# Batch norm with ReLU on one core: which two rows are computed in two parts

## The chip, the cores and the metric

One core of a Trainium2 chip. The metric is device microseconds of one execution. The traced span of an execution, from its first to its last instruction, is about 1.7 us shorter than its time (82.0 against 83.68); one kernel below (e1) differs.

## The reference

```python
def reference(x, gamma, beta, running_mean, running_var, eps):   # x: (32, 128, 32, 32) float32
    normalized = (x - running_mean[None, :, None, None]) / np.sqrt(running_var[None, :, None, None] + eps)
    scaled = normalized * gamma[None, :, None, None] + beta[None, :, None, None]
    return np.maximum(scaled, 0).astype(np.float32)
```

x is 16.78 MB; it is read once and a result of the same size is written once.

## The kernel before

x is seen as two halves t, each of 128 partitions times 16 rows j times 1024 elements. The 16 rows of a partition are 64 KB that lie together in memory. All of x fits on the chip, so every tile has a place of its own and no buffer is reused. `TILES` lists the tiles as (half, first row, end row). A tile is one load, except that the second half is loaded in two (`LOAD_CUTS`), and one store, except that the first tile is stored row by row (`STORE_CUTS`).

```python
J = 16
TILES = ((0, 0, 2), (0, 2, 4), (0, 4, 8), (0, 8, 16), (1, 0, 16))
LOAD_CUTS = {(1, 8)}
STORE_CUTS = {(0, 1)}
HALVES = {(0, 0), (0, 1)}
# ...
    tiles = []
    for t, a, b in TILES:                          # six loads, all issued from SP
        xt = data.tile([P, b - a, HW], F32, name=f"x{t}_{a}")
        cuts = [a] + [j for j in range(a + 1, b) if (t, j) in LOAD_CUTS] + [b]
        for c, d in zip(cuts, cuts[1:]):
            nc.sync.dma_start(out=xt[:, c - a : d - a, :], in_=xr[t, :, c:d, :])
        tiles.append((t, a, b, xt))
# ... the parameters: four tiny loads, a matmul that spreads them, sqrt, reciprocal, scale_t, bias_t
    with tc.manual_schedule(engines={mybir.EngineType.Activation}):
        for t, a, b, xt in tiles:
            first = a
            for j in range(a, b):
                step = HW // 2 if (t, j) in HALVES else HW
                for w in range(0, HW, step):
                    nc.scalar.activation(
                        out=xt[:, j - a, w : w + step], in_=xt[:, j - a, w : w + step],
                        func=ACTF.Relu, bias=bias_t[:, j : j + 1], scale=scale_t[:, j : j + 1],
                    )
                if j + 1 == b or (t, j + 1) in STORE_CUTS:
                    nc.scalar.dma_start(
                        out=outr[t, :, first : j + 1, :], in_=xt[:, first - a : j + 1 - a, :]
                    )
                    first = j + 1
```

So ACT (ScalarE) computes every row and also issues the six stores; SP issues the six loads.

## Time and profile before

| | before |
|---|---|
| time, median of 3 (range) | 83.6 us (83.53 to 83.6) |
| span of the profiled run | 82.0 us |
| ACT busy | 39.1 us (48%) |
| load queue q1, store queue q10, share of the 16 DMA engines' span | 48.7%, 47.6% |
| bytes read, written | 16.78 MB, 16.78 MB |

The prediction below shows the lines that carry the reading. (A load brings data from memory to the core, a store takes it back; 16 DMA engines move both. A packet is the unit that the trace records: here one partition's stretch of a transfer, 4 to 64 KB, and a few very small ones.) A queue's share times the span is the time that each DMA engine spent on that queue's packets: 48.7% of 82.0 is 39.9 us for loads, 47.6% is 39.0 us for stores, and the rest, 3.0 us, is time in which the engine had no packet. **Span = loads + stores + rest** is an account in which a lost microsecond must show up in one of three columns. (Shares are printed to 0.1%, so loads and stores are each good to 0.05 us and the rest to 0.1. Packets overlap a little in the records, which show up to 16.8 of 16 engines busy at a time.)

Two lines of the list of DMA issues and one of the waits give the slack behind ACT (the last number of an issue is the time from issue to landing; for a wait: total, times, longest, in us):

```profile
out_dram<-x ACTq DMA_DIRECT2D x1, 4096.0 KB, 28.7
out_dram<-x ACTq DMA_DIRECT2D x1, 25.1
...
ACT x L102 <- DMA x<-in_x_dram: 7.6, 3, 2.9
```

The first is the 4 MB store, the second the last store, whose size is not printed.

### The profile page before, as it was taken

How to read it: one execution, taken by the hardware profiler on the slowest of the kernel's cores; microseconds unless marked ns; L12 is line 12 of the kernel's file. 1: busy time of each engine (PE TensorE's matmuls, PEld its weight loads, DVE VectorE, ACT ScalarE, POOL GpSimd, SP SyncE). 2: the span in 40 equal slices, each digit the busy share in tenths (PEclk: the TensorE clock that was granted, in tenths of full speed). 3: DMA queues.
4: the chain of work that ended last, by engine and by line, in shares of the span. 5: the costliest groups of instructions: out<-in, count | busy, mean ns of one | idle time of the engine just before them, and what ended most of it. 6: DMA issues, size and time to landing. Idle time of an engine off the chain costs nothing.

```text
span 82.0 us, 120 instructions
## 1 busy us (share of the span) xinstructions
PE 0.7 (1%) x2; PEld 0.5 (1%) x2; DVE 0.8 (1%) x5; ACT 39.1 (48%) x36; POOL 0.8 (1%) x6
## 2 busy tenths in 40 slices
PE   0002000000000000000000000000000000000000
PEld 0002000000000000000000000000000000000000
DVE  0000300000000000000000000000000000000000
ACT  0600477799239999199994199993000000000000
POOL 3000000000000000000000000000000000000000
DMA  2899997979899989999799799998992999996590
GB/s 48 336 424 456 416 544 336 524 322 526 338 434 430 506 358 506 390 434 444 320 460 500 316 424 448 512 432 368 480 736 128 416 512 512 512 512 288 224 512 0
DMA packets 1792, 33.56 MB, mean 409 GB/s; under 512 B 256, under 2 KB 256, under 8 KB 512
## 3 DMA queue, kind: packets, MB, share of 16 engines
q1 hardware_dynamic: 864, 16.78, 48.7%
q10 hardware_dynamic: 928, 16.78, 47.6%
HBM read 16.78 MB, written 16.78 MB: 409 GB/s over the span
## 4 chain that ended last, share of the span: by engine, by line
DMA 56%; ACT 10%; issue 2%; SPq 0%
DMA x<-in_x_dram 56%; ACT x L102 10%; SPq L56 0%
## 5 line engine op out<-in xcount | busy, mean ns | idle before, releaser
L102 ACT ACTIVATE x<-x,bias_t,scale_t 128x1024 f32<-128x1024 f32 (+1 forms) x34 | 37.5, 1177 | 9.9 <-DMA x<-in_x_dram 7.6
L86 ACT ACT_TABLE_LOAD x1 | 1.3, 1283 | 2.6 <-issue 2.6
L86 ACT ACTIVATE std_t<-cols,eps_t 128x16 f32<-128x16 f32 x1 | 0.3, 273 | 4.5 <-PE cols L78 4.5
L78 PE MATMUL cols<-raw,rep 8*128 8x64 f32 x2 | 0.7, 429 | 7.6 <-DMA raw<-in_beta_dram 7.6
L78 PEld LDWEIGHTS cols<-raw,rep 8*128 8x128 f32 x2 | 0.5, 306 | 7.6 <-issue 7.6
L68 POOL TENSOR_SCALAR_AFFINE_SELECT rep<-rep 8x128 f32<-8x128 f32 x1 | 0.4, 392 | 0.1
L88 DVE RECIPROCAL rstd_t<-std_t 128x16 f32<-128x16 f32 x1 | 0.3, 254 | 7.7 <-ACT std_t L86 7.7
L67 POOL MEMSET rep<- 8x128 f32 x1 | 0.2, 194 | 0.3 <-POOLq L130 0.3
L90 DVE TENSOR_TENSOR scale_t<-cols,rstd_t 128x16 f32<-128x16 f32 x1 | 0.2, 175 | 0.1
L92 DVE TENSOR_TENSOR ms_t<-cols,scale_t 128x16 f32<-128x16 f32 x1 | 0.2, 175 | 0.0
L94 DVE TENSOR_TENSOR bias_t<-cols,ms_t 128x16 f32<-128x16 f32 x1 | 0.2, 174 | 0.0
L130 POOL MEMSET const-bfloat16-1.0<- 128x1 bf16 x1 | 0.1, 106 | 0.0
L130 POOL MEMSET const-uint8-127<- 128x1 uint8 x1 | 0.1, 106 | 0.0
L130 POOL MEMSET const-float32-0.0<- 128x1 f32 x1 | 0.1, 103 | 0.3 <-issue 0.3
L130 POOL MEMSET const-float32-1.0<- 128x1 f32 x1 | 0.1, 103 | 0.0
L65 DVE MEMSET eps_t<- 128x1 f32 x1 | 0.1, 59 | 0.9 <-PEq L130 0.9
## 6 DMA issues: line engine op xcount, KB each, us to landing
x<-in_x_dram SPq DMA_DIRECT2D x3, 4096.0 KB, 38.7
out_dram<-x ACTq DMA_DIRECT2D x1, 4096.0 KB, 28.7
x<-in_x_dram SPq DMA_DIRECT2D x2, 1024.0 KB, 5.8
x<-in_x_dram SPq DMA_DIRECT2D x1, 2048.0 KB, 11.3
out_dram<-x ACTq DMA_DIRECT2D x1, 2048.0 KB
out_dram<-x ACTq DMA_DIRECT2D x2, 512.0 KB, 19.6
out_dram<-x ACTq DMA_DIRECT2D x1, 1024.0 KB
raw<-in_running_var_dram ACTq DMA_DIRECT2D x1, 0.5 KB
```

The source lines that it names most:

```text
L65: nc.vector.memset(eps_t, float(eps))
L67: nc.gpsimd.memset(rep, 1.0)
L68: nc.gpsimd.affine_select(out=rep, in_=rep, compare_op=mybir.AluOpType.is_equal, fill=0.0, base=0, pattern=[[0, P // Q], [-1, Q]], channel ...
L78: nc.tensor.matmul(cols.rearrange("p k j -> p (k j)"), rep.rearrange("q r s -> q (r s)"), raw.rearrange("q k j -> q (k j)"), start=True, s ...
L86: nc.scalar.activation(out=std_t, in_=cols[:, 0, :], func=ACTF.Sqrt, bias=eps_t[:, 0:1], scale=1.0)
L88: nc.vector.reciprocal(out=rstd_t, in_=std_t)
L90: nc.vector.tensor_mul(out=scale_t, in0=cols[:, 1, :], in1=rstd_t)
L92: nc.vector.tensor_mul(out=ms_t, in0=cols[:, 2, :], in1=scale_t)
L94: nc.vector.tensor_sub(out=bias_t, in0=cols[:, 3, :], in1=ms_t)
L102: nc.scalar.activation(out=xt[:, j - a, w : w + step], in_=xt[:, j - a, w : w + step], func=ACTF.Relu, bias=bias_t[:, j : j + 1], scale=sc ...
L130: nc = _bacc.Bacc("TRN2", target_bir_lowering=False, num_devices=1)
```

## The change

The two split rows move from the start of ACT's work to the middle of it. In itself the split costs ACT time; at the start it delays the first stores, in the second half it stands ahead of a wait for a load. The numbers that are computed stay the same.

```diff
-HALVES = {(0, 0), (0, 1)}
+HALVES = {(1, 0), (1, 1)}
```

## The prediction

> **What bounds the kernel now.** I read the page's slices first, then its queue lines, then the timeline of ScalarE (ACT), the DMA windows, and last the waits. The kernel does one fused scale, bias and relu per row of x on ACT, in place, between a stream of loads on one DMA queue (q1) and a stream of stores on another (q10). From the page of the kernel before (busy tenths in 40 slices of about 2.05 us, then the queues with packets, MB and the share of the 16 DMA engines' span):
>
> ```profile
> ACT  0600477799239999199994199993000000000000
> DMA  2899997979899989999799799998992999996590
> q1 hardware_dynamic: 864, 16.78, 48.7%
> q10 hardware_dynamic: 928, 16.78, 47.6%
> ```
>
> The DMA row is nearly full from the second slice to the last but two. The two queues add up to 96.3% of 82.0 us, which is 79.0 us of work for each engine, so only 3.0 us are left without a packet. ACT has 39.1 us of work (48%) and nothing at all in the last twelve slices. Is the 3.0 us at the ends or in the middle? From the windows (columns: stretch, its length, busy times of five engines, clock, DMA share, GB/s):
>
> ```profile
> 0.00:2.20 2.20, 0.00 (x0) 0.00 (x0) 0.06 (x1) 0.00 (x0) 0.80 (x6) 1.00 0.30 56
> 2.20:11.20 9.00, 0.66 (x2) 0.50 (x2) 0.78 (x4) 3.07 (x4) 0.00 (x0) 1.00 1.00 420
> 11.20:46.90 35.70, 0.00 (x0) 0.00 (x0) 0.00 (x0) 26.87 (x25) 0.00 (x0) 1.00 1.01 426
> 46.90:81.10 34.20, 0.00 (x0) 0.00 (x0) 0.00 (x0) 9.12 (x8) 0.00 (x0) 1.00 0.98 423
> 81.10:82.00 0.90, 0.00 (x0) 0.00 (x0) 0.00 (x0) 0.00 (x0) 0.00 (x0) 1.00 0.00 0
> ```
>
> At the ends: the start (2.2 us at a share of 0.30, so about 1.5 us idle) and the last 0.9 us. In the three stretches between, the share is 1.00, 1.01 and 0.98 (a packet seems to be booked whole where it starts, hence the 1.01 and the uneven tenths of short slices), and the rate is 420, 426 and 423 GB/s whether only loads run, both run, or only stores run. So the DMA engines never starve between 2.2 and 81.1 us, and how loads and stores are mixed changes the rate by under 2%. **The bound is bytes over DMA rate**: 33.56 MB at about 425 GB/s is 79 us, plus the two ends.
>
> Now where ACT stands against this, in the timeline (start, length, then work and, in brackets, the idle time before it and what ended it):
>
> ```profile
> 9.61 1.52 ACT L102 ACTIVATE x<-x,bias_t,scale_t 128x512 f32<-128x512 f32 x2 [1.02 <-DVE bias_t L94]
> 11.16 0.37 ACTq L110 DMA_DIRECT2D out_dram<-x  x1
> 11.58 1.52 ACT L102 ACTIVATE x<-x,bias_t,scale_t 128x512 f32<-128x512 f32 x2 [0.45 <-ACT x L102]
> 13.13 0.37 ACTq L110 DMA_DIRECT2D out_dram<-x  x1
> ...
> 23.91 9.16 ACT L102 ACTIVATE x<-x,bias_t,scale_t 128x1024 f32<-128x1024 f32 x8 [2.94 <-DMA x<-in_x_dram]
> ...
> 34.85 9.16 ACT L102 ACTIVATE x<-x,bias_t,scale_t 128x1024 f32<-128x1024 f32 x8 [1.78 <-DMA x<-in_x_dram]
> 46.87 9.16 ACT L102 ACTIVATE x<-x,bias_t,scale_t 128x1024 f32<-128x1024 f32 x8 [2.86 <-DMA x<-in_x_dram]
> 56.05 0.34 ACTq L110 DMA_DIRECT2D out_dram<-x  x1
> ```
>
> (Left out: rows 2 to 7 of the first half with their stores at 15.95 and 21.00, and the 4 MB store at 33.10.) Three times ACT waits for a load: before 23.91, 34.85 and 46.87. Those waits, 2.94 + 1.78 + 2.86 = 7.6 us, are the total that the view of waits gives. They are cushions: ACT work that grows or shrinks ahead of one is taken up by it. The last store is issued at 56.05. The list of DMA issues gives the 4 MB store ahead of it, issued at 33.10, a landing 28.7 us later, at 61.8. So the store queue has work for 61.8 - 56.1 = 5.7 us more when the last store joins it; that store lands 25.1 us after its issue, at 81.2, and the rest of the span is the closing.
>
> **What the Trainium skill says.** "DMA: Bandwidth & Descriptors", section "Where 436 GB/s comes from", puts a ceiling of 435.2 GB/s on the 16 ports; the trace's 420 to 426 agrees that little is left. The same page, section "Queues, rings and completion order", says that each DMA engine goes round its queues packet by packet. The trace agrees: 864 packets on q1 are 6 loads x 128 partitions plus 6 x 16 small ones, so a packet is one partition's run (8, 16 or 32 KB for loads, 4 to 64 KB for stores). While both run, the first 24 store packets of an engine (8 x 4, 8 x 4, 8 x 8 KB) facing 24 load packets of 32 KB would give 768 to 128 KB, 6 to 1; the queue view for 11.2 to 46.9 us has 12.88 MB loaded and 2.33 MB stored, 5.5 to 1. "ScalarE: Activation LUTs", section "What ACT_TABLE_LOAD costs", gives 280 ns + 0.833 ns per element for an ACTIVATE with one pointer operand and about 93 ns more for a second (ours has scale and bias): 800 ns at 512 and 1226 ns at 1024. The groups by form show 805 and 1227 ns on average. It agrees.
>
> **The change part by part.** The two rows split into two instructions of 512 elements become rows 0 and 1 of the second half of x; instruction count, bytes, transfers and buffers stay as they are.
>
> Removed at the front: a pair of halves takes 1.52 us, one whole row 1.23 us, so 0.29 us less for row 0 and the same for row 1. The first store should be issued at 11.16 - 0.29 = 10.87, the second at 13.13 - 0.58 = 12.55, the third (rows 2 and 3) at 15.95 - 0.58 = 15.37 and the fourth (rows 4 to 7) at about 20.4. No load holds these back: the 2 MB load of rows 4 to 7 is issued by 2.3 us and lands 11.3 us later, by 13.6, while its rows would start at 15.76. Then ACT waits for the load of rows 8 to 15 as before; the 2.94 us wait becomes about 3.5. The 0.58 us ends there.
>
> Added at the back: inside a run of rows, a row adds (9.16 - 1.23) / 7 = 1.13 us; a half adds 1.52 - 0.81 = 0.71, so a split row 1.42. Two of them make the run that starts at 34.85 longer by 2 x 0.29 = 0.58 us: it ends at 44.6 instead of 44.0. The load that lets the last eight rows go arrives at 46.87, so the wait shrinks from 2.86 to about 2.3. There is no store between rows 7 and 8 of that half, so nothing is issued later. The last store goes out at 56.05 as before.
>
> DMA: starting stores 0.3 to 0.6 us earlier moves at most a round or so of store packets forward. One round is a 4 or 8 KB packet, 0.15 or 0.30 us at 425/16 = 26.6 GB/s for an engine. Loads may therefore land up to 0.3 us later, the last run may start at 46.9 to 47.2, and the last store be issued at 56.1 to 56.4, still over 5 us before the store queue is empty. What moves forward in the store queue is paid back after the loads end. Sum on the path that sets the end: 0.0 us. Sum of ACT busy time: -0.58 + 0.58 = 0.
>
> **The rivals.** First, the front sets the time: each store that leaves earlier shortens everything after it. That would make 83.6 - 0.6 = 83.0 us (-0.7%). For it: the first store can't start before ACT. Against it: the engines are full with loads meanwhile (share 1.00 from 2.2 to 11.2 us), so an earlier store only displaces a load. Second, the back sets the time: the extra 0.58 us reaches the last store and the end, 84.2 us (+0.7%). For it: the chain of waits does run through the last eight ACT rows. Against it: two cushions, 2.86 us and 5.7 us, each larger than 0.58. Third, the mixing: stores that join earlier change how reads and writes interleave, and mixed traffic is slower or faster. Against it: 420, 426 and 423 GB/s in the three stretches; a shift of 0.6 us at a rate that differs by 1.5% is 0.01 us. I see no engine that could become the bound: ACT stays at 39.1 us.
>
> **Range and chances.** The working says no change, so 83.6 us. The three times of before lie between 83.53 and 83.6 and the profiled run took 83.68, so the scatter is about 0.1 us; I widen to 83.3 to 83.9 for chip-to-chip scatter and for half of either of the first two rivals. Even a rival in full is 0.7%, far inside 2%: within 2% has 0.98, the other two 0.01 each.
>
> **What would show it right or wrong.** Right: the first store issued near 10.9, the wait before the rows 8 to 15 of the first half about 0.6 us longer, that before the last eight rows 0.3 to 0.6 us shorter, their start at 46.8 to 47.2, the last store issued before 56.5 and landing near 81.2, queue shares still 96 to 97%, ACT busy 39.1 us. Wrong: an idle DMA stretch in the middle, a start of the last rows moved by more than 0.5 us, a last store that leaves after the 4 MB store has landed, or a store-only rate other than 423 GB/s with all else the same; the last would mean that how loads and stores meet costs time, the term that I put at zero.

## The result, and the profile after

The changed kernel took 83.51 us (median of 6, 83.44 to 83.59) and the kernel before 83.56 us (median of 6, 83.48 to 83.71). The ratio was 0.9993 with a 95% interval of 0.998 to 1.0006: no change. (A ratio is the mean time of one kernel's runs over the mean of the other's of the same rounds, so it is not quite the ratio of the medians quoted.) The output was correct.

From the page of the changed kernel (busy tenths in 40 slices, then the queues):

```profile
ACT  0600477799039999199998099993000000000000
DMA  2899999999989898969789699996993899999090
q1 hardware_dynamic: 864, 16.78, 48.5%
q10 hardware_dynamic: 928, 16.78, 47.7%
```

From its timeline (start, length, work, idle time before it):

```profile
9.63 1.24 ACT L102 ACTIVATE x<-x,bias_t,scale_t 128x1024 f32<-128x1024 f32 x1 [1.02 <-DVE bias_t L94]
10.90 0.37 ACTq L110 DMA_DIRECT2D out_dram<-x  x1
11.32 1.24 ACT L102 ACTIVATE x<-x,bias_t,scale_t 128x1024 f32<-128x1024 f32 x1 [0.45 <-ACT x L102]
12.59 0.37 ACTq L110 DMA_DIRECT2D out_dram<-x  x1
...
23.85 9.16 ACT L102 ACTIVATE x<-x,bias_t,scale_t 128x1024 f32<-128x1024 f32 x8 [3.42 <-DMA x<-in_x_dram]
...
34.92 9.71 ACT L102 ACTIVATE x<-x,bias_t,scale_t 128x512 f32<-128x512 f32 x10 [1.92 <-DMA x<-in_x_dram]
46.91 9.16 ACT L102 ACTIVATE x<-x,bias_t,scale_t 128x1024 f32<-128x1024 f32 x8 [2.27 <-DMA x<-in_x_dram]
56.09 0.34 ACTq L110 DMA_DIRECT2D out_dram<-x  x1
```

And from its waits and its list of issues (the last store):

```profile
ACT x L102 <- DMA x<-in_x_dram: 7.6, 3, 3.4
```

```profile
out_dram<-x ACTq DMA_DIRECT2D x1, 25.0
```

The reader is to see the 0.55 us wander. It leaves the front: the second store goes out at 12.59 in place of 13.13 us. It is swallowed by the first wait, 3.42 in place of 2.94 us. It comes back in the second half: that group of ten instructions (four halves and six rows, listed under its first form) takes 9.71 in place of 9.16 us. It is swallowed again by the last wait, 2.27 in place of 2.86 us. The total of the three waits is 7.6 us in both kernels, the last rows start at 46.91 against 46.87, the last store leaves at 56.09 against 56.05 and lands at 81.1 against 81.2. The account is 39.7 + 39.1 + 3.1 us against 39.9 + 39.0 + 3.0.

### The profile page after: what moved, and what is told of

Its sections match the earlier page's. It is cut to its first block, busy times and chain, and to the rows that moved or that the text cites. A ratio compares the mean times of both kernels' runs of the same rounds, so it can differ in the third digit from the quotient of the medians. Undisturbed runs are those within 1.5% of the kernel's fastest.

```text
span 81.9 us, 120 instructions
## 1 busy us (share of the span) xinstructions
PE 0.7 (1%) x2; PEld 0.5 (1%) x2; DVE 0.8 (1%) x5; ACT 39.1 (48%) x36; POOL 0.8 (1%) x6
## 4 chain that ended last, share of the span: by engine, by line
DMA 56%; ACT 10%; issue 2%; SPq 0%
DMA x<-in_x_dram 56%; ACT x L102 10%; SPq L56 0%
## 5 line engine op out<-in xcount | busy, mean ns | idle before, releaser
L102 ACT ACTIVATE x<-x,bias_t,scale_t 128x1024 f32<-128x1024 f32 (+1 forms) x34 | 37.5, 1178 | 9.9 <-DMA x<-in_x_dram 7.6
```

What stands on the lines that cost most here:

```text
L102: nc.scalar.activation(out=xt[:, j - a, w : w + step], in_=xt[:, j - a, w : w + step], func=ACTF.Relu, bias=bias_t[:, j : j + 1], scale=sc ...
```

## The experiments

That nothing happened is weak evidence for a reason: a change that could not matter and one that was absorbed look the same. So the experiments make ACT's delay large, put it where one cushion or the other must take it, and move the stores in time. The theory is that of the prediction: the time is the DMA engines' packets plus their idle time, and ACT has cushions. The rivals are that the front sets the time, that the back does, and that how loads and stores meet costs time. All diffs are against the changed kernel. Ratios are to the kernel before, run on the same chip. All outputs were correct.

The account of every profiled run, from its shares and span, with the mean length of its 32 KB load packets, worked out from the packet records of the trace:

| run | time, median us | ratio (95%) | loads + stores + rest = span | 32 KB load packet, mean (longest) us |
|---|---|---|---|---|
| before, first profile | 83.56 | | 39.9 + 39.0 + 3.0 = 82.0 | 1.233 (1.46) |
| changed, first profile | 83.51 | 0.9993 (0.998 to 1.0006) | 39.7 + 39.1 + 3.1 = 81.9 | 1.223 (1.48) |
| e1_no_halves | 83.99 | 1.0032 (1.0005 to 1.006) | 39.8 + 39.0 + 3.3 = 82.1 | 1.232 (1.57) |
| e2_halves_last_rows | 83.57 | 0.9983 (0.9956 to 1.001) | 39.8 + 39.1 + 3.0 = 81.9 | 1.234 (1.43) |
| e3_front_16 | 84.19 | 1.0057 (1.002 to 1.0094) | 40.2 + 39.1 + 3.1 = 82.4 | 1.253 (1.67) |
| e4_last_rows_16 | 87.77 | 1.0486 (1.0452 to 1.0519) | 39.8 + 39.2 + 7.1 = 86.1 | 1.229 (1.40) |
| e5_back_16 | 84.69 | 1.0129 (1.0107 to 1.0152) | 39.6 + 39.1 + 4.1 = 82.9 | 1.224 (1.46) |
| e6_stores_late | 84.39 | 1.0095 (1.0072 to 1.0118) | 40.4 + 39.0 + 3.2 = 82.7 | 1.258 (2.04) |
| e7_big_both | 83.87 | 1.0031 (1.0012 to 1.0051) | 39.6 + 38.8 + 3.9 = 82.3 | 1.219 (1.33) |
| e8_front_16_stores_late | 84.25 | 1.0079 (1.006 to 1.0098) | 40.2 + 39.1 + 3.1 = 82.4 | 1.244 (1.91) |
| e9_big_cut | 85.06 | 1.0186 (1.0166 to 1.0206) | 40.6 + 38.8 + 3.8 = 83.2 | 1.287 (2.43) |
| e10_after_again | 83.55 | 1.0007 (0.9988 to 1.0027) | 39.9 + 39.0 + 3.3 = 82.2 | 1.230 (1.55) |
| e11_before_again | 83.93 (one look) | | 39.8 + 39.0 + 3.4 = 82.2 | 1.229 (1.83) |
| e12_one_store_late | 85.14 | 1.0193 (1.0176 to 1.021) | 39.5 + 38.9 + 5.2 = 83.6 | 1.214 (1.22) |

### e1_no_halves: no split at all

```diff
-HALVES = {(1, 0), (1, 1)}
+HALVES = set()
```

> No row is split: the front as in the changed kernel, the back as in the kernel before, so ACT has two fewer instructions and 0.58 us less work than either. Theory (DMA bytes bound, ACT changes absorbed by waits): same time as both, 83.5 us within 0.2; last store issued near 56.1; the wait before the last eight rows back to about 2.85 us. Rival front (earlier first stores shorten the run, and the changed kernel paid that back by its later halves): 83.0 us, that is -0.6.

Measured: 83.99 us against 83.78 for before, whose eleven runs spread from 83.44 to 84.0. Less work came out 0.3% slower, and the expected 83.5 was missed. But the traced spans of its six runs lie between 81.8 and 82.1 us, on average 81.95, against 82.03 for the eleven runs of before. What is longer is the difference of time and span: 2.02 to 2.09 us in all six runs, where every run of every other kernel has 1.66 to 1.76. So the split rows cost or save nothing in the span, and this program has about 0.34 us more outside the span, of which the trace shows nothing. The rival front (83.0 us) is refuted at its own size: the front was as in the changed kernel, the back as in the kernel before, and the span did not shrink by 0.6. The last store left at 56.05 us and the wait before the last rows was 2.84 us, as expected.

### e2_halves_last_rows: the split behind the last wait

```diff
-HALVES = {(1, 0), (1, 1)}
+HALVES = {(1, 8), (1, 9)}
```

> The two split rows are rows 8 and 9 of the second half, after the last wait for a load, where only the store queue's backlog (5.7 us) can absorb them. Theory: last store issued 0.58 us later than in the changed kernel, 56.7 us, the time unchanged, 83.5 within 0.2, the last store landing at the same 81.1. Rival back: +0.58 us, 84.1.

From its timeline and its list of issues:

```profile
46.94 9.71 ACT L102 ACTIVATE x<-x,bias_t,scale_t 128x512 f32<-128x512 f32 x10 [2.96 <-DMA x<-in_x_dram]
56.68 0.34 ACTq L110 DMA_DIRECT2D out_dram<-x  x1
```

```profile
out_dram<-x ACTq DMA_DIRECT2D x1, 24.4
```

The last store left 0.6 us later, at 56.68, took 0.6 us less to land (24.4 in place of 25.0) and landed at the same 81.1 us. Time 83.57 us. This is the second cushion at work alone: the store waits in its queue behind the 4 MB store anyway.

### e4_last_rows_16 and e5_back_16: more than the cushions hold

e4 splits rows 8 and 9 of the second half, e5 rows 0 and 1 of it (no change to `HALVES`), in 16 parts each:

```diff
-HALVES = {(1, 0), (1, 1)}
+HALVES = {(1, 8), (1, 9)}            # e4 alone
-                step = HW // 2 if (t, j) in HALVES else HW
+                step = HW // 16 if (t, j) in HALVES else HW
```

> Rows 8 and 9 of the second half in 16 parts each: 8.7 us more ACT work after the last wait for a load, a dose beyond the 5.7 us of backlog. Theory: last store issued near 64.8, after the store queue has run dry at about 61.7; the DMA engines idle from there until the last store's first packet, some 1.4 us after its issue (the first load's packets come that long after its issue), so 4.5 us of idle DMA in the middle and a time of 88.0, with 1 us either way. If the backlog were no real cushion: +8.7, 92.2. If ACT were not on the path at all: 83.5.

> Rows 0 and 1 of the second half (the rows the change picked) in 16 parts each: 8.7 us more than whole rows, ahead of the last wait for a load. Theory: that wait (2.85 us with whole rows) goes to zero, the last eight rows start 5.8 us late at 52.7, the last store leaves at 61.9, its first packet about 1.1 us later (64.5 to 65.6 us in the run with rows 8 and 9 in 16 parts), 63.0, against a store queue dry at 61.7: 1.3 us of idle DMA, time 84.8 us, between 84.3 and 85.5. Without the first cushion it would be the 87.8 of that other run.

The timeline of e4 and its windows (stretch, length, busy times, clock, DMA share, GB/s):

```profile
46.89 17.57 ACT L102 ACTIVATE x<-x,bias_t,scale_t 128x64 f32<-128x64 f32 x38 [2.81 <-DMA x<-in_x_dram]
64.49 0.34 ACTq L110 DMA_DIRECT2D out_dram<-x  x1
```

```profile
62.00:65.00 3.00, 0.00 (x0) 0.00 (x0) 0.00 (x0) 2.46 (x3) 0.00 (x0) 1.00 0.00 0
```

The timeline of e5:

```profile
34.80 26.54 ACT L102 ACTIVATE x<-x,bias_t,scale_t 128x64 f32<-128x64 f32 x46 [1.80 <-DMA x<-in_x_dram]
61.37 0.34 ACTq L110 DMA_DIRECT2D out_dram<-x  x1
```

The dose is nearly the same, 8.4 us (17.57 less 9.16) in e4. In e4 only the store queue's backlog can take it, and in the 3 us shown no packet starts: the engines are dry while ACT is still computing. (By the packet records none moves from 61.50 to 65.33 us.) In e5 the wait for the load is gone (rows 0 to 15 run as one group of 26.54 us), and the last store leaves at 61.37 us, just as the queue runs dry. Measured 87.77 and 84.69 us, expected 88.0 and 84.8. In the account both add to the rest alone: 4.0 to 4.1 us and 1.0 to 1.1 us. So both cushions are real, and what exceeds them was paid in idle DMA time. Their sizes follow: in e4 the backlog took 8.4 - 4.0 = 4.4 us; in e5, whose dose is 8.3 us (26.54 less 18.24 for sixteen whole rows, as e3 below shows), the wait of 2.8 us and the backlog took 8.3 - 1.1 = 7.2, which leaves 4.4 again. The wait has the size read before; the backlog is smaller than the 5.7 us read from its landing, because its last packet had ended by 61.5 us and the last store's first packet started only 0.84 us after its issue. (The two expectations had allowed 1.4 and 1.1 us for this.) The rival back is true only beyond the cushions; for the change's 0.55 us it is refuted.

### e3_front_16: a large delay at the front

```diff
-HALVES = {(1, 0), (1, 1)}
+HALVES = {(0, 0), (0, 1)}
-                step = HW // 2 if (t, j) in HALVES else HW
+                step = HW // 16 if (t, j) in HALVES else HW
```

> Rows 0 and 1 of the first half in 16 parts each. A part of 64 costs about 0.34 us (from 1.13 us a row and 0.71 a half in a run: 0.29 fixed and 0.05 for 64 elements), so each row 5.5 us in place of 1.13 and ACT is 8.7 us later at the front. Theory: the three waits for loads (3.4, 1.9, 2.3 us, 7.6 in all) take up 7.6 us, the last rows start about 1.1 us later, near 48, the last store leaves near 57.2, still before the backlog ends: time unchanged, 83.5 within 0.3. Rival front: a delay of the first store is paid, +8.7 us, 92; if stores that start later only lengthen the store-only stretch at the same rate, nothing.

Its timeline and its queues:

```profile
29.37 9.18 ACT L102 ACTIVATE x<-x,bias_t,scale_t 128x1024 f32<-128x1024 f32 x8 [0.42 <-ACT x L102]
...
38.96 18.24 ACT L102 ACTIVATE x<-x,bias_t,scale_t 128x1024 f32<-128x1024 f32 x16 [0.41 <-ACT x L102]
57.23 0.34 ACTq L110 DMA_DIRECT2D out_dram<-x  x1
```

```profile
q1 hardware_dynamic: 864, 16.78, 48.8%
q10 hardware_dynamic: 928, 16.78, 47.4%
```

All three waits for loads are gone, and the last store leaves at 57.23 us, 1.1 us later, as expected. The time was to stay; it was 84.19 us, 0.6% above before. The 8.5 us of delay were not paid, so the rival front is refuted again, but 0.4 us were. The account puts them in the loads: 40.2 us, with the rest still 3.1. No engine idled in the middle; the load packets took longer, most of it (0.5 us for each engine above 1.21 us a packet, by the packet records) between 40 and 44 us, just after the 4 MB store was issued at 38.58 us.

### e6_stores_late and e8_front_16_stores_late: the first half's stores held back

e6 (e8 uses `(0, 15)` in place of `(1, 4)`, and has the front in 16 parts as e3):

```diff
+        held = []
         for t, a, b, xt in tiles:
# ...
-                    nc.scalar.dma_start(out=..., in_=...)
+                    if t == 0:
+                        held.append((outr[t, :, first : j + 1, :], xt[:, first - a : j + 1 - a, :]))
+                    else:
+                        nc.scalar.dma_start(out=..., in_=...)
                     first = j + 1
+                if (t, j) == (1, 4):
+                    for o, i in held:
+                        nc.scalar.dma_start(out=o, in_=i)
```

> The five stores of the first half are held back by up to 27 us, until row 4 of the second half is done, near 37.6 us, so that loads run almost alone (to about 42 us) and then stores almost alone. Theory (bytes over rate, when a store starts doesn't matter while the engines have packets): 83.5 us within 0.3, no idle DMA. Rival front: 83.5 + 27 = 110. Rival mixing (loads and stores in turn slow each other, as the 0.4 us of the run with the front in 16 parts suggests, where load packets of 32 KB took 1.25 us in place of 1.22): about 0.3 to 0.5 us faster, 83.1.

> The front in 16 parts as in the run that came out at 84.2, but the five first-half stores held until row 15 of the first half is done, near 37.3 us. If the 0.4 us there came from ACT's delay as such: 0.4 above the run with held stores and unsplit front. If it came from how store packets met load packets: the same as that run, within 0.2 us, and load packets of 32 KB at 1.22 us on average, not 1.25.

From the timeline of e6, and its DMA view for 38.5 to 42.0 us; then the same view of the changed kernel (queue, packets, MB, share of the 16 engines in that stretch):

```profile
32.39 0.86 ACTq L120 DMA_DIRECT2D out_dram<-x  x2
```

```profile
q1 hardware_dynamic: 32, 1.05, 98.1%
q10 hardware_dynamic: 32, 0.13, 9.1%
```

```profile
q1 hardware_dynamic: 47, 1.54, 101.9%
q10 hardware_dynamic: 33, 0.27, 18.2%
```

Two expectations failed. First, the place: the stores were issued from 32.39 us, not 37.6, when the first of the second half's rows had just started: here the issue ran ahead of the ACT instructions before it in the program. In e8 the stores went out from 22.81 us, ahead of the ACT work in the same way, but not before their own rows were done (the 4 MB store at 36.03, its last row at 36.00). The first store packets came at 14.4 to 14.8 us in before, 19.0 to 19.5 in e3, 26.5 to 27.0 in e8 and 36.0 to 36.5 in e6. Second, the sign: holding the stores back was neither free nor a gain but cost 0.95% in e6 and 0.8% in e8. Some 22 us of delay of the first store cost 0.8 us, so the front is still not the bound. And e8, with 8.5 us more ACT work ahead of the stores, is not slower than e6. But its stores also went out earlier than those of e6, and its load packets averaged 1.244 us, not the expected 1.22, so the pair does not separate ACT's delay from the meeting of loads and stores as planned.

What does cost shows in the fences. In 3.5 us e6 took 32 load packets of 32 KB for 98.1% of 16 engines' time: 0.981 x 3.5 x 16 / 32 = 1.72 us each. The changed kernel took 47 in the same stretch: 1.019 x 3.5 x 16 / 47 = 1.21 us each, though it moved more store bytes beside them. The slow packets came late: beside the first store packets, at 36.3 to 38.5 us, load packets still took 1.21 to 1.28. Over the run the mean packet is 1.258 us in e6 against 1.23 in four looks at the two kernels. An engine has 24 such packets, so that is 24 x 0.03 = 0.7 us of the 0.8. (In e8 it is 24 x 0.015 = 0.4 us of 0.7.)

### e7_big_both and e9_big_cut: fewer, larger transfers

```diff
-TILES = ((0, 0, 2), (0, 2, 4), (0, 4, 8), (0, 8, 16), (1, 0, 16))
+TILES = ((0, 0, 16), (1, 0, 16))
-STORE_CUTS = {(0, 1)}
+STORE_CUTS = set()                   # e9: {(0, 12)}
-HALVES = {(1, 0), (1, 1)}
+HALVES = set()
```

> First half loaded in one 64 KB packet a partition and stored likewise, second half as it was, no split rows. Packets took 0.34 us (8 KB load), 0.61 (16 KB), 1.22 (32 KB), and 0.16, 0.31, 0.61, 1.21 (4 to 32 KB stores) against 2.42 for 64 KB; per engine 8 of each: loads save about 0.7 us, stores 0.3. ACT starts at 21.5 and the first store leaves near 40, when the loads are nearly done; the last store leaves near 59 against a first store that ends near 60, so no idle expected, but little room. Theory: 82.6 us, 0.9 below the changed kernel, between 82.2 and 83.2. If an early first store mattered (rival front): 83.5 + 29 or so.

> The kernel with 64 KB loads of the first half, but its store is cut after row 11, so that the first store is issued near 36.5 us and not at 41.1. In the uncut kernel the loads were done about 0.5 us before the first store's packets came, and its DMA engines had 78.5 us of packets in 79.2 us: 0.7 us idle. Theory (bytes over rate, idle costs one for one): the idle goes, 83.2 us, 0.6 below the uncut kernel and 0.3 below the changed kernel. Rival mixing: the one or two rounds in which loads and stores now meet take back 0.3 us or more, 83.5 or above.

These were tries at a version that beats both kernels, and both missed. e7 came to 83.87 us, not 82.6: loads and stores shrank by 0.3 and 0.2 us against before, less than I had summed from the packet lengths, and the rest grew by 0.9. By the packet records the first 64 KB load packet of each engine took 3.1 us on average and the later ones 2.43, so their mean was 2.51 and not 2.42: 8 x 0.09 = 0.7 us, the saving expected. e9 was to win back the rest and came to 85.06 us, not 83.2. The idle time of 0.5 us between 36 and 46 us did go, but the rest hardly shrank (3.8 us), because the engines then idled 2.0 us at the end of the span, against 1.5 in e7; why, I have not found. And the loads grew by 1.0 us to 40.6. The DMA view of e9 for 37.5 to 40.9 us tells where:

```profile
DMA packets 33, 1.08 MB, mean 318 GB/s; under 512 B 0, under 2 KB 0, under 8 KB 0
...
q1 hardware_dynamic: 33, 1.08, 106.3%
```

33 load packets took 1.063 x 3.4 x 16 / 33 = 1.75 us each, and there is no store packet in the stretch; a store had been issued at 36.66 us, and its first packet came after 41.0. So load packets are slow here while a store is queued, before its first packet is recorded; up to the issue at 36.66 us they had taken 1.21. Small store packets, which I had supposed after e6, are therefore not needed for it.

### e12_one_store_late: one large store, meeting few loads

```diff
-TILES = ((0, 0, 2), (0, 2, 4), (0, 4, 8), (0, 8, 16), (1, 0, 16))
+TILES = ((0, 0, 16), (1, 0, 16))
-LOAD_CUTS = {(1, 8)}
-STORE_CUTS = {(0, 1)}
-HALVES = {(1, 0), (1, 1)}
+LOAD_CUTS = {(0, 2), (0, 4), (0, 8), (1, 8)}
+STORE_CUTS = set()
+HALVES = set()
# and the stores of the first half held back as in e6, with (1, 10)
```

> Loads as in the kernel before, no split rows, but the first half goes out in one 64 KB store, placed so that it is issued near 36 us and its packets come near 40, when one or two rounds of loads are left. Tells what made the run with five small stores held back 0.8 us slow. Theory: small store packets that meet the last loads slow these down (load packets of 1.5 to 2.0 us there); with 64 KB store packets few rounds meet and the loss is under 0.3 us: 83.1 us, between 82.8 and 83.5. Rival: holding stores back as such costs 0.8 us, 84.4.

The hold was misplaced again. The store was issued at 42.31 us, when row 8 of the second half had started, after the loads were done, so loads and stores never met. It does not answer its question about large packets, but it is the run without a meeting. Every 32 KB load packet took 1.21 to 1.22 us, the loads 39.5 us, the least of all kernels with these load sizes. And it is slow, 85.14 us, because the rest is 5.2 us. The DMA view for 40 to 44 us (busy tenths in 40 slices of 0.1 us, a packet booked where it starts) shows the gap:

```profile
DMA  7999070000000000000000000000000999000000
```

The last load packet starts near 40.5 us and takes 1.2 us, the first store packets start at 43.1 to 43.4 us: some 1.4 us in which no engine moves data. Most engines were done sooner, between 40.4 and 41.8 us, so the mean gap of an engine is 1.8 us. So 0.4 us is won from the loads, and about 2 us go into the rest, nearly all of it this gap.

### e10_after_again and e11_before_again: the two kernels once more

> The changed kernel once more, unedited, beside the kernel before. Theory: no difference, ratio 1.000 within 0.003, and the busy DMA time of the two profiles scatters by 0.2 to 0.3 us either way from look to look. If the change itself saves DMA time, as its first profile (load packets 0.2 us per engine less than the first profile of before) would allow: the saving is there again.

> The kernel before once more, for a second profile of it. Theory: its queue shares and 32 KB load packets scatter as those of the others do: mean packet between 1.22 and 1.24 us; the first profile's 1.233 against 1.223 for the changed kernel is scatter, not the change.

The first two profiles differed by 0.2 us in the loads (39.9 and 39.7), in favour of the change. The second look has 39.9 for the changed kernel and 39.8 for before, with mean packets of 1.230 and 1.229 us. So the difference was scatter. The ratio of e10 was 1.0007, with an interval from 0.9988 to 1.0027. (e11 is a single look at 83.93 us; its span, 82.2, is that of e10's profiled run.)

## Why the prediction was right

**The bound is bytes over DMA rate: right.** In the account, loads and stores together stay between 78.4 and 79.5 us in all fourteen profiles, and the large losses of e4, e5 and e12 sit in the rest. One reading was off: the prediction placed 1.5 + 0.9 = 2.4 of the 3.0 us at the ends, from shares that book a packet where it starts. By the packets' starts and ends the engines of the kernel before idled 2.0 us at the start and 1.4 at the end (3.4, less the 0.4 of overlap between packets), and not in the middle. There the prediction's conclusion holds.

**The front gives 0.58 us to ACT and nothing to the time: right.** Stores at 10.90 and 12.59 us were predicted as 10.87 and 12.55, the first wait as about 3.5 and was 3.42. e3 shows that even 8.5 us there are not paid as such.

**The back costs ACT 0.58 us and the time nothing: right, and tested beyond.** The last wait was put at about 2.3 and was 2.27. e2, e4 and e5 measure the two cushions: 0.6 us is absorbed by the second alone, and a dose of about 8.4 us costs 4.0 us or 1.1 us, depending on which cushions it meets. The second was read too large, 5.7 us where e4 and e5 show 4.4; against 0.58 us this did not matter.

**The first store's delay and the loads' landing: right.** The last rows started at 46.91 us, inside 46.8 to 47.2.

**The mixing rival, put at 0.01 us: right for this change, too small as a view.** I argued from three stretches at 420, 426 and 423 GB/s that mixing costs under 2%. That holds for this kernel, but the cost depends on when the stores come: 0.6%, 0.8% and 0.95% in e3, e8 and e6, for first store packets 4.7, 12 and 22 us later (the other stores moved too). The change moves the first store by 0.26 us; at the steepest of these slopes, 0.6% for 4.7 us, that is an estimate of 0.03 us, below the scatter. The kernel is not indifferent to when its stores start, but the change hardly moves that.

**What stays open.** Why load packets stretch from 1.21 to as much as 2.4 us at some times while stores are queued. They do so with 4 KB stores (e6), with 48 KB stores (e9), and before the first store packet (e9), but not beside the first store packets of e6; they don't where no store is queued (e12). Whether it is in the memory, in the DMA engines or at their ports, these traces don't tell. Open too is what makes up the extra 0.34 us outside the span of e1.

No kernel tried here beats the two: the fastest of the others, e2, has their time.

## What to carry to other kernels

Before you move work about on an engine, follow it to the next wait for a transfer and to the queue behind the last transfer: what was shorter than those cushions moved nothing here. Keep an account of DMA time as loads, stores and rest; it tells a late issue (rest grows) from slow packets (loads grow) at a glance. And when a run differs by a few tenths of a microsecond, compare spans as well as times.

## What the Trainium skill lacked or had wrong

- "DMA: Bandwidth & Descriptors", section "Queues, rings and completion order": it has the turns by packet, which the queue view agrees with, but not what follows for two queues: the shares go by packet length. Here loads moved 12.88 MB and stores 2.33 MB between 11.2 and 46.9 us, mostly in packets of 32 KB against 4 to 16 KB; between 15.5 and 40 us, 277 load and 287 store packets of 4 KB or more started.
- The same page's first-byte latency for the sync and scalar queues, about 0.6 us ("Latency and other measured facts"), is near what idle engines showed: the last store of e4, issued at 64.49 us, had its first packet at 65.33, which is 0.84 us after the start of the issue and 0.50 after its end. With a full load queue it was 3.4 us (before: issued at 11.16, first packet at 14.60 us). The page lacks this case.
- No page that I read has it that load packets can slow down while stores are queued on the other queue: 32 KB packets took 1.21 to 1.22 us with no store queued (e12) and up to 2.43 us otherwise (e9).
- No page that I read has it that the time outside the traced span can differ by program: 2.02 to 2.09 us for e1 (six runs), 1.66 to 1.76 us for all others.
